# Two queue edits in a decoder layer: mixed rows split inside the output projection, operand differences started at the last scaling

## The chip, the cores and the metric

The kernel runs on one core of a Trainium2 chip. The metric is the device time of one execution in microseconds (us); lower is better. The core has five engines with a queue each, and each runs its queue in order: TensorE (PE in the profile) for matmuls, VectorE (DVE) and ScalarE (ACT) for elementwise work, GpSimd (POOL) for elementwise work in SBUF, and SyncE (SP), which here issues the DMAs.

## The reference

One layer of a hybrid decoder with D = 1024, run on 1024 prompt positions and 64 sampled ones (1088 rows together). Four retention heads and four mLSTM heads share one input projection; their gated outputs are concatenated, projected, normalised and added to the residual; a gated feed-forward part with a causal convolution of width 3 follows.

```python
proj = (rmsnorm(x, pre_mix_g) @ w_in).astype(f32)     # q, k, v, gates of both head groups
...
ret_y = head_groupnorm(ret_out, ret_g) * jax.nn.silu(g_r)
ml_y = head_groupnorm(ml_out, ml_g) * jax.nn.sigmoid(o_m)
mix = jnp.concatenate([ret_y, ml_y], axis=-1) @ w_out
x = x + rmsnorm(mix, post_mix_g)
h2 = rmsnorm(x, pre_ffn_g)
up = h2 @ w_up                                        # 2 * D_FF = 5632 columns
padded = jnp.concatenate([conv_buf, up], axis=1)
conv = sum(padded[:, j:j + L] * conv_w[j] for j in range(CONV_W)) + conv_b
gate, val = conv[..., :D_FF], conv[..., D_FF:]
ffn = (jax.nn.gelu(gate, approximate=True) * val) @ w_down
x = x + rmsnorm(ffn, post_ffn_g)
```

All inputs and outputs are float32. The states of both head groups and the convolution rows are outputs too.

## The kernel before

Rows are kept transposed: 128 features on the partitions, rows along the free axis. The 1088 rows are cut into four quarters of 272, numbered 0 to 3, and every matmul of the large projections has 128x128 weights and 272 columns. Each product is done in three matmuls: operand and weight are split into a high part (a copy rounded to a shorter float, on ACT) and a low part (the difference, on DVE), and high times high, low times high and high times low are summed in PSUM. `split_to` writes one ACT and one DVE instruction for that (profile lines L144 and L146), and leaves them in `last["split"]`.

The order of the instructions on each engine comes from a scheduler that places them by the order of the program and by when it thinks their operands are ready. `tc.issue_after(ins)` forces what is written inside it behind `ins` on that instruction's engine. Tiles with one tag share their space: a new one waits until every reader of the old one is done.

**From the mixer to the output projection.** The eight heads' results lie in `yT` (four tiles of two heads each, tags f0 to f3). The last four input projections make the late gates; `late_gate` multiplies a gate into `yT` (L497, the sigmoid L499, the product L500). With the last of them, `last_gate(b)` runs after each quarter b: it splits the finished rows of `yT` into the operand `mx` (`mix_split`, four ACT and four DVE instructions a quarter, tiles `mh` and `ml`), and at b = 1 and b = 3 it loads and splits the first two weight tiles of the output projection. Then the pools of the mixer are closed, and new tiles take their space.

`out_proj(b)` runs the output projection of one quarter: eight tiles of 128 features (`m` = 0 to 7), each with 24 matmuls (L165, tile `out`). `load_wo` loads and splits one weight tile ahead of each, with two more ahead of the first. The result is evacuated by ACT into `mo` (L861, which takes the tags f0 to f3 of `yT`), its square is summed into `oacc` (L863 on ACT, L865 on DVE). After each of the eight a step from a list is run: between the groups of one quarter the norm, the residual and the scaling of the quarter before are written (`post_mix`: `first`, two `residual`, `scale`). `rstd_block` is a norm: a matmul with ones over the partitions (L192, tiles `ssqb_po` and `ssqb_pf`), then L193 to L198 on DVE and ACT. `scale` multiplies eight tiles of a quarter by the norm (L899).

**The up-projection.** The first two column blocks (`PLAIN` = 2, j = 0 and 1) are done as plain products of the four quarters (`plain`, L1070 to L1072), in an order written by hand that is shown at the end of the code; the other 20 blocks use a Strassen form with seven products for eight (`product`, names A11, A12, S1 to S4, A22; L1026 to L1028). Its operands are the four parts of the scaled rows, B1 to B4 (by feature half and row half), and four combinations, T1 to T4. `first_half` and `second_half` split B1, B2 and B4, B3. `combine(i, eng)` writes the differences in place in `mo`, for one half of the columns each (L915 to L918): `combine(0, gpsimd)` has all four on POOL, `combine(1, vector)` has two on DVE and two on POOL. T2, T1, T3 and T4 are then split from `mo`. The result of block j goes into two tiles U (`Ug`, `Uv`), by L1011, L1000 and L1004 out of PSUM; `pair_out` runs the convolution over them (`conv`, L1034 to L1041, into tile `c`, which takes the space of the `mo` tile that T2 is split from), the gelu and the product. There are two sets of U tiles, so block j + 2 waits for the convolution of block j. Eight PSUM banks serve all products in turn.

Four products of the third block (A11 and A12, two column halves each) are run ahead and held in PSUM, until the U tiles of the first block are free. `weight_prep(j)` loads and splits the weights of block j; four pairs of weight tiles go round.

Of the kernel before, what the change touches and what calls it, by code (L numbers as in the profile page):

```python
# [10 lines left out]
F32 = mybir.dt.float32  # L11
# [3 lines left out]
ALU = mybir.AluOpType  # L15

P = 128
# [24 lines left out]
V_PREMIX, V_POSTMIX, V_PREFFN, V_POSTFFN, V_HEAD = 0, 8, 16, 24, 32  # L42
# [50 lines left out]
def hybrid_layer_kernel(ctx: ExitStack, tc: tile.TileContext, a: dict, o: dict):  # L93
    nc = tc.nc
# [8 lines left out]
    last = {}  # L103

    cp = pool("cp", bufs=1)
# [4 lines left out]
    def slot(i, name, dt=F32R):  # L110

        return (bigp if i < 8 else fp).tile([P, 4, 2 * Q], dt, tag=f"x{i}", bufs=1, name=name)

    def quadrants(name, th):

        return [tuple(slot(4 * th + 2 * kh + i, f"{name}{'hl'[i]}_{th}{kh}") for i in range(2)) for kh in range(2)]

    def qcols(b):
        return slice(Q * (b % 2), Q * (b % 2) + Q)
# [6 lines left out]
    def bank(p, cols, name, rows=P, dt=F32):  # L126
        t = p.tile([P, 512], dt, tag="bank", name=name)
        return t[:rows, :cols]
# [12 lines left out]
    def split_to(x, hi, lo, eng=nc.vector, after=None):  # L141
        act, dve = after or (None, None)
        with tc.issue_after(act.ins) if act else nullcontext():
            act = nc.scalar.activation(hi, x, AF.Copy)  # L144
        with tc.issue_after(dve.ins) if dve and eng is nc.vector else nullcontext():
            last["split"] = act, eng.tensor_tensor(lo, x, hi.bitcast(F32), ALU.subtract)  # L146
        return hi, lo

    def load_w(src, name, p=None, tag="w"):
        return split_w(stage_w(src, name), name, p, tag)  # L150
# [29 lines left out]
    vec = cp.tile([P, V_N], F32, name="vec")  # L180
# [36 lines left out]
    def xcols(b):  # L217
        o0, n = BLK[b]
        return a["x"][:, KT * o0:KT * (o0 + n)].rearrange("p (k n) -> p k n", k=KT)
# [560 lines left out]
    def mix_split(b, after=None):  # L780
        if b % 2 == 0:
            mx.append(quadrants("m", b // 2))
        o0, n = BLK[b]
        for k in range(0, KT, 2):
            hi, lo = (t[:, k % 4:k % 4 + 2, qcols(b)] for t in mx[b // 2][k // 4])
            x = yT[k // 2][:, :, o0:o0 + n]
            split_to(x, hi, lo, nc.vector, after)
# [6 lines left out]
    def last_gate(b):  # L794
        if b in (1, 3):
            wo.append(load_w(a["wo"][b // 2], f"out{b // 2}"))
            after = last["split"]
        for i in ((0,), (1,), (), (2, 3))[b]:
            mix_split(i, after if i > 1 else None)

    proj((31, late_gate(7)), done=last_gate)
    log_exp_tables(last["sigmoid"])
# [29 lines left out]
    def load_wo():  # L832

        m = len(wo)
        if m >= KT:
            return
        if m in (4, 6):
            wx.extend(slot(m + 4 + i, f"wo{'hl'[i]}{m}").rearrange("p k n -> p (k n)") for i in range(2))
        if m not in (4, 5):
            st = stage_w(a["wo"][m], f"out{m}")  # L840
        else:
            st = utile(f"st_out{m}", 0)[:, :D]
            nc.sync.dma_start(st, a["wo"][m])
        if m < 4:
            wo.append(split_w(st, f"out{m}", *wtile()))
        else:
            wo.append(split_to(st, *(t[:, m % 2 * D:(m % 2 + 1) * D] for t in wx[-2:])))
# [4 lines left out]
    def out_proj(b, steps=()):  # L852
        steps = list(steps)
        t = ttile(f"oacc{b}")
        acc, *sq = (t[:, i * Q:(i + 1) * Q] for i in range(3))
        for i in range(KT):
            m = (i + 4 * (b == 3)) % KT
            load_wo()
            ps = bank(psA, Q, f"out{m}_{b}")
            dense(ps, wo[m], mx, b)  # L860
            nc.scalar.activation(quarter(m // 4, b)[:, m % 4, :], ps, AF.Copy,  # L861
                                 scale=vec[:, V_POSTMIX + m:V_POSTMIX + m + 1])
            last["sq"] = nc.scalar.activation(sq[i % 2] if i else acc, ps, AF.Square)  # L863
            if i:
                last["acc"] = nc.vector.tensor_tensor(acc, acc, sq[i % 2], ALU.add)  # L865
            if steps:
                steps.pop(0)()
        for f in steps:
            f()
        return [acc, *sq]  # L870

    def post_mix(b, t):

        xr, st = [], {}

        def first():
            for kh in range(2):
                x = slot(6 + kh, f"xr{kh}_{b}", F32).rearrange("p k n -> p (k n)") if b == 3 else utile(f"xr{kh}_{b}", 1)
                x = x[:, :4 * Q].rearrange("p (k n) -> p k n", k=4)
                nc.sync.dma_start(x, xcols(b)[:, 4 * kh:4 * kh + 4, :])  # L880
                xr.append(x)
            st["r"] = t[1]
            rstd_block(t[0], t[1], t[2], t[0], f"po{b}", last.get("fill"))

        def residual(kh):
            m = quarter(kh, b)
            nc.vector.tensor_tensor(m, m, st["r"].unsqueeze(1).broadcast_to([P, 4, Q]), ALU.mult)
            (nc.gpsimd if kh and b == 3 else nc.vector).tensor_tensor(m, m, xr[kh], ALU.add)
            nc.scalar.activation(xr[kh], m, AF.Square)
            nc.sync.dma_start(x1cols(b)[:, 4 * kh:4 * kh + 4, :], m)  # L890
            nc.vector.tensor_tensor(xr[kh][:, :2], xr[kh][:, :2], xr[kh][:, 2:], ALU.add)

        def scale():
            nc.vector.tensor_tensor(xr[0][:, :2], xr[0][:, :2], xr[1][:, :2], ALU.add)
            nc.vector.tensor_tensor(xr[0][:, 0], xr[0][:, 0], xr[0][:, 1], ALU.add)
            rstd_block(xr[0][:, 0], t[1], t[2], t[0], f"pf{b}", last.get("fill"))
            for k in range(KT):
                m = quarter(k // 4, b)[:, k % 4, :]
                nc.vector.scalar_tensor_tensor(m, m, vec[:, V_PREFFN + k:V_PREFFN + k + 1], st["r"],  # L899
                                               ALU.mult, ALU.mult)  # L900

        return [first, lambda: residual(0), lambda: residual(1), scale]

# [8 lines left out]

    def combine(i, eng):
        q = {(kh, th): mo[kh][th][:, :, qcols(i)] for kh in range(2) for th in range(2)}
        eng.tensor_tensor(q[0, 0], q[0, 1], q[0, 0], ALU.subtract)  # L915
        nc.gpsimd.tensor_tensor(q[0, 1], q[1, 1], q[0, 1], ALU.subtract)
        eng.tensor_tensor(q[1, 1], q[1, 1], q[0, 0], ALU.subtract)
        nc.gpsimd.tensor_tensor(q[1, 0], q[1, 0], q[1, 1], ALU.subtract)  # L918
# [12 lines left out]

    skip = lambda: None
    spaced = lambda f: [f[0], skip, f[1], f[2], skip, f[3]]
    acc = out_proj(0)
    acc = out_proj(1, spaced(post_mix(0, acc)))
    acc = out_proj(2, spaced(post_mix(1, acc)) + [lambda: first_half(0)])
    acc = out_proj(3, spaced(post_mix(2, acc)) + [lambda: first_half(1)])


    cache = fp.tile([P, 2 * JT, 9, 2], F32, bufs=1, name="cache")  # L940
    nc.sync.dma_start(cache, a["cache"].rearrange("p (j s t) -> p j s t", j=2 * JT, s=9))
    seq = lambda v: v.rearrange("p (s t) -> p s t", s=NB)

    def weight_prep(j):

        plain = j < PLAIN
        ws = {}

        def parts(i, x, *names):
            p, tag = wtile()  # L950
            n = len(names) * D // 2
            hi = p.tile([P, D], F32R, tag=tag + "hi", name=f"wh_up{j}_{i}")[:, :n]
            lo = p.tile([P, D], F32R, tag=tag + "lo", name=f"wl_up{j}_{i}")[:, :n]
            split_to(x, hi, lo, nc.vector, (last["sq"], last["acc"]) if i in (1, 2) else None)
            for c, name in enumerate(names):
                cols = slice(c * D // 2, (c + 1) * D // 2)
                ws[name] = hi[:, cols], lo[:, cols]

        parts(0, stage_w(a["wu"][j, 0], f"up{j}_0"), "A11", "A12")
        if plain:  # L960
            parts(3, stage_w(a["wu"][j, 1], f"up{j}_1"), "A22", "A21")
            yield ws
            return
        yield ws
        sums = sd[j].rearrange("p b n -> p (b n)")
        for i, names in ((1, ("S1", "S2")), (2, ("S4", "S3"))):
            parts(i, stage_w(sums[:, (i - 1) * D:i * D], f"up{j}_{i}"), *names)
            yield
        st = fp.tile([P, D // 2], F32, tag="s1", bufs=1, name=f"st_up{j}_3")
        nc.sync.dma_start(st, a["wu"][j, 1][:, :D // 2])  # L970
        parts(3, st, "A22")
        yield
# [255 lines left out]
    acc = [t_acc[b // 2][:, b % 2 * Q:(b % 2 + 1) * Q] for b in range(4)]  # L1228
# [171 lines left out]
```

## Time and profile before

| what | value |
|---|---|
| median of three runs | 1375.17 us (1373.82 to 1376.09) |
| the profiled execution | 1375.41 us, of it 1373.6 us from the first to the last instruction |
| PE busy | 1348.8 us, 98% of the span |
| DVE, ACT, POOL busy | 1009.7, 596.3, 440.8 us (74%, 43%, 32%) |
| mean granted TensorE clock | 0.993 |
| last input projection ends, output projection starts | 541.05 and 541.67 us |
| output projection ends, first plain product starts | 646.56 us |
| first held product of the third block | 700.58 us |

Busy time of PE counts pipelined matmuls from start to end, so that it can be near 100% while matmuls start at different rates; the granted clock tells slow ones from fast ones. In the rows of instructions, the first number is the start in us after the first instruction, the second the time from the start of the first to the end of the last of the group, `xN` their number, and a bracket tells how long the engine was idle before and what released it. In the rows of waits stand the waiting engine and line, what it waited for, and total us, times and the longest.

### The profile page before, as it was taken

How to read it: one execution, taken by the hardware profiler on the slowest of the kernel's cores; microseconds unless marked ns; L12 is line 12 of the kernel's file. 1: busy time of each engine (PE TensorE's matmuls, PEld its weight loads, DVE VectorE, ACT ScalarE, POOL GpSimd, SP SyncE). 2: the span in 40 equal slices, each digit the busy share in tenths (PEclk: the TensorE clock that was granted, in tenths of full speed). 3: DMA queues.
4: the chain of work that ended last, by engine and by line, in shares of the span. 5: the costliest groups of instructions: out<-in, count | busy, mean ns of one | idle time of the engine just before them, and what ended most of it. 6: DMA issues, size and time to landing. Idle time of an engine off the chain costs nothing.

```text
span 1373.6 us, 26916 instructions
## 1 busy us (share of the span) xinstructions
PE 1348.8 (98%) x10583; PEld 1323.9 (96%) x10583; DVE 1009.7 (74%) x2013; ACT 596.3 (43%) x1107; POOL 440.8 (32%) x567
## 2 busy tenths in 40 slices
PE   9999999999999999999999999999999999999995
PEld 8999999999999999999899999999999999999995
DVE  6778775556465366568899978778778789995677
ACT  8444433212222235446364434434344455453652
POOL 0344440577775000000353322221222205872000
PEclk9999999999999999999999999999999999999998
DMA  6433442478784211432123444443444359533363
GB/s 242 134 113 123 159 156 64 157 212 192 227 186 156 64 34 48 158 116 97 64 93 135 163 143 136 135 132 116 142 150 141 135 158 334 175 95 95 92 212 130
DMA packets 93166, 192.80 MB, mean 140 GB/s; under 512 B 16240, under 2 KB 41456, under 8 KB 92528
## 3 DMA queue, kind: packets, MB, share of 16 engines
q1 hardware_dynamic: 80736, 149.03, 33.2%
q0 software_dynamic: 12160, 41.95, 10.7%
q8 instruction: 83, 1.36, 0.4%
q14 instruction: 43, 0.35, 0.1%
q10 hardware_dynamic: 144, 0.11, 0.0%
HBM read 134.58 MB, written 56.47 MB: 139 GB/s over the span
## 4 chain that ended last, share of the span: by engine, by line
PE 90%; DVE 4%; ACT 3%; DMA 1%; issue 1%; SPq 0%; DVEq 0%; ACTq 0%
PE in L165 27%; PE up_S L1028 6%; PE out L165 6%; PE up_S L1027 6%; PE up_S L1026 6%; PE dn L1223 5%; PE dn L1225 5%; PE dn L1224 4%; PE up_A L1027 4%; PE up_A L1026 4%; PE up_A L1028 4%; ACT hh L205 1%; PE up_A L1071 1%; PE up_A L1072 1%; PE up_A L1070 1%
## 5 line engine op out<-in xcount | busy, mean ns | idle before, releaser
L165 PE MATMUL in<-hh,wh_in 128*128 128x272 f32 x1024 | 299.7, 294 | 1.7 <-ACT v_r L453 1.5
L165 PE MATMUL in<-hh,wl_in 128*128 128x272 f32 x1024 | 295.9, 291 | 0.0
L165 PE MATMUL in<-hl,wh_in 128*128 128x272 f32 x1024 | 295.2, 291 | 0.0
L165 PEld LDWEIGHTS in<-hh,wh_in 128*128 128x128 f32 x1024 | 192.3, 188 | 5.8 <-issue 2.0
L165 PEld LDWEIGHTS in<-hh,wl_in 128*128 128x128 f32 x1024 | 192.2, 189 | 3.8 <-issue 3.5
L165 PEld LDWEIGHTS in<-hl,wh_in 128*128 128x128 f32 x1024 | 191.7, 188 | 1.6 <-issue 1.5
L144 ACT ACTIVATE wh_up<-st_up 128x1024 fp32r<-128x1024 f32 x84 | 80.6, 960 | 160.6 <-PE up_S L1027 98.3
L146 DVE TENSOR_TENSOR wl_up<-st_up,wh_up 128x1024 fp32r<-128x1024 f32 x84 | 95.8, 1141 | 8.9 <-ACT wh_up L144 8.9
L1000 DVE TENSOR_TENSOR Uv<-Uv,up_S 128x272 f32<-128x272 f32 (+1 forms) x200 | 66.4, 374 | 46.1 <-PE up_S L1028 46.1
L1152 DVE TENSOR_TENSOR rb<-rb 128x544 fp32r<-128x544 f32 x78 | 74.3, 957 | 34.2 <-ACT rb L1151 33.7
L736 POOL TENSOR_TENSOR tab<-tab 128x256 f32<-128x256 f32 x104 | 84.1, 819 | 9.3 <-DMA tab<-in_wu 4.7
L1172 POOL TENSOR_TENSOR wd<-wd 128x512 f32<-128x512 f32 x44 | 72.3, 1669 | 34.6 <-DMA wd<-in_wd 20.8
L1151 ACT ACTIVATE rb<-rb 128x544 fp32r<-128x544 f32 x78 | 50.5, 650 | 74.3 <-DMA rb<-bd 70.2
L1056 POOL TENSOR_TENSOR act<-act 128x544 f32<-128x544 f32 x40 | 63.1, 1577 | 61.0 <-DMA bd<-act 33.1
L991 POOL MEMSET Ug<- 128x2 f32 x22 | 2.2, 100 | 234.4 <-DMA xr<-in_x 121.8
L1041 DVE SCALAR_TENSOR_TENSOR c<-Uv,vec,c 128x1024 f32<-128x1024 f32 (+1 forms) x88 | 70.0, 798 | 9.1 <-ACT c L1039 9.1
L1041 DVE SCALAR_TENSOR_TENSOR c<-Ug,vec,c 128x1024 f32<-128x1024 f32 x88 | 67.5, 805 | 1.2 <-ACT c L1039 1.2
L736 POOL TENSOR_TENSOR wq<-wq 128x256 f32<-128x256 f32 x56 | 50.3, 908 | 48.3 <-DMA wq<-in_wu 46.1
L1039 ACT ACTIVATE c<-Ug,vec 128x1024 f32<-128x1024 f32 (+1 forms) x44 | 34.6, 834 | 53.6 <-DVE Ug L1004 47.4
L736 POOL DMA_DIRECT2D tab<-in_wu x52 | 36.8, 714 | 61.7 <-DVE k_r L468 44.0
L146 DVE TENSOR_TENSOR wl_in<-st_in,wh_in 128x1024 fp32r<-128x1024 f32 (+2 forms) x33 | 40.5, 1226 | 13.5 <-ACT wh_in L144 13.4
L1028 PE MATMUL up_S<-T1h,wl_up 128*128 128x272 f32 x160 | 46.4, 290 | 0.0
(548 smaller groups left out, 4668.0 us busy)
## 6 DMA issues: line engine op xcount, KB each, us to landing
rb<-bd SPq DMA_DIRECT2D x76, 272.0 KB, 2.9
st_up<-sd SPq DMA_DIRECT2D x40, 512.0 KB, 4.0
bd<-act SPq DMA_DIRECT2D x33, 544.0 KB, 3.9
st_in<-in_wi SPq DMA_DIRECT2D x31, 512.0 KB, 3.8
tab<-in_wu POOLq DMA_DIRECT2D x52, 256.0 KB, 4.6
sd<-tab POOLq DMA_DIRECT2D x26, 512.0 KB, 3.5
st_up<-in_wu SPq DMA_DIRECT2D x24, 512.0 KB, 3.3
wd<-in_wd SPq DMA_DIRECT2D x44, 256.0 KB, 4.8
```

The lines of the kernel that those rows point to most:

```text
L144: act = nc.scalar.activation(hi, x, AF.Copy)
L146: last["split"] = act, eng.tensor_tensor(lo, x, hi.bitcast(F32), ALU.subtract)
L165: nc.tensor.matmul(ps, u[:, ws], v, start=k == i == 0, stop=k == KT - 1 and i == 2)
L736: last["sums"] = f(*args)
L1026: nc.tensor.matmul(ps, wh[:, c], xh[:, k, n], start=k == 0, stop=False)
L1027: nc.tensor.matmul(ps, wh[:, c], xl[:, k, n], start=False, stop=False)
L1028: nc.tensor.matmul(ps, wl[:, c], xh[:, k, n], start=False, stop=k == 3)
L1041: nc.vector.scalar_tensor_tensor(c, u(i), cw(i), c, ALU.mult, ALU.add)
L1152: nc.vector.tensor_tensor(lo, x, hi.bitcast(F32), ALU.subtract)
L1172: nc.gpsimd.tensor_tensor(quad(p, out), quad(p, x), quad(p, y), op)
L1223: nc.tensor.matmul(t, wh[:, ms], ah, start=k == 0, stop=False)
L1225: last["dn"] = nc.tensor.matmul(t, wl[:, ms], ah, start=False, stop=k == KH - 1)
```

## The change

The splits of the mixed rows of quarters 2 and 3 are taken out of `last_gate`. They become steps of `out_proj(0)`: quarter 2 after its first group of 24 matmuls, by when five weight tiles of the output projection have been written in the program, and behind the last of their splits on ACT and DVE; quarter 3 after its third group, with no order forced. `last_gate` keeps the splits of quarters 0 and 1 and the loads of two weight tiles.

`scale` of the last quarter now leaves its last scaling in `last["acc"]`, and is followed by one instruction on POOL, over one column of a tile `hold`, that reads the last scaled rows (`last["gate"]`). The first difference of `combine(0)` is ordered behind that instruction on POOL, the first of `combine(1)` behind the last scaling on DVE; the splits that were ordered behind `last["acc"]` and are written later (B4 and B3 of the second column half, T1 to T4, and weights of the third and later blocks) now stand behind the last scaling too, instead of the last sum of `out_proj(3)`.

The weight splits of block j = 1 are ordered behind the last square of `out_proj(3)` on ACT and its last sum on DVE.

No matmul, DMA or split is added or taken away; one small POOL instruction is added.

```diff
     def last_gate(b):
         if b in (1, 3):
             wo.append(load_w(a["wo"][b // 2], f"out{b // 2}"))
-            after = last["split"]
-        for i in ((0,), (1,), (), (2, 3))[b]:
-            mix_split(i, after if i > 1 else None)
+        if b < 2:
+            mix_split(b)
...
             for k in range(KT):
                 m = quarter(k // 4, b)[:, k % 4, :]
-                nc.vector.scalar_tensor_tensor(m, m, vec[:, V_PREFFN + k:V_PREFFN + k + 1], st["r"],
-                                               ALU.mult, ALU.mult)
+                d = nc.vector.scalar_tensor_tensor(m, m, vec[:, V_PREFFN + k:V_PREFFN + k + 1], st["r"],
+                                                   ALU.mult, ALU.mult)
+            if b == 3:
+                last["acc"] = d
+                last["gate"] = nc.gpsimd.tensor_tensor(hold, m[:, :1], m[:, 1:2], ALU.subtract)
...
     def combine(i, eng):
         q = {(kh, th): mo[kh][th][:, :, qcols(i)] for kh in range(2) for th in range(2)}
-        eng.tensor_tensor(q[0, 0], q[0, 1], q[0, 0], ALU.subtract)
+        with tc.issue_after(last["gate" if eng is nc.gpsimd else "acc"].ins):
+            eng.tensor_tensor(q[0, 0], q[0, 1], q[0, 0], ALU.subtract)
...
-    acc = out_proj(0)
+    acc = out_proj(0, [lambda: mix_split(2, last["split"]), skip, lambda: mix_split(3)])
...
+    hold = cp.tile([P, 1], F32, name="hold")
...
-            split_to(x, hi, lo, nc.vector, (last["sq"], last["acc"]) if i in (1, 2) else None)
+            split_to(x, hi, lo, nc.vector, (last["sq"], last["acc"]) if i in (1, 2) or j == 1 else None)
```

The hand-written order behind which the differences stand:

```python
for j in range(PLAIN):
    begin_plain(j)
plain(*firsts[0], 0)
norm()
second_half(0)
plain(*firsts[0], 1)
add0()
add1()
plain(*firsts[0], 2)
plain(*firsts[1], 0)
scale()
second_half(1)
plain(*firsts[1], 1)
plain(*firsts[1], 2)
for f in firsts:
    plain(*f, 3)
...
held = [product(name, i) for name in ("A11", "A12") for i in range(2)]
for i, e in ((0, nc.gpsimd), (1, nc.vector)):
    combine(i, e)
```

## The prediction

> **What bounds the kernel now.** I read the page first (busy shares, the chain), then who PE waited for, then the stretches round the two places of the edit, then the instructions of DVE, ACT and POOL there.
>
> ```profile
> span 1373.6 us, 26916 instructions
> PE 1348.8 (98%) x10583; PEld 1323.9 (96%) x10583; DVE 1009.7 (74%) x2013; ACT 596.3 (43%) x1107; POOL 440.8 (32%) x567
> PE 90%; DVE 4%; ACT 3%; DMA 1%; issue 1%; SPq 0%; DVEq 0%; ACTq 0%
> ```
>
> PE is the bound, and the chain of waits runs over it. So a change elsewhere can only give back what PE loses near it: its waits, and the slow matmuls behind them. PE's waits between 500 and 720 us, and stretches (columns: length, then busy us and count of PE, PEld, DVE, ACT, POOL, granted clock, DMA share, GB/s):
>
> ```profile
> PE out L165 <- ACT wh_out L144: 2.6, 2, 2.1
> PE ssqb_po L192 <- DVE oacc L865: 2.3, 2, 1.8
> PE ssqb_pf L192 <- DVE xr L895: 1.1, 1, 1.1
> ...
> 541.60:573.75 32.15, 29.46 (x216) 28.91 (x216) 0.95 0.47 171
> ...
> 652.70:662.65 9.95, 8.15 (x51) 7.87 (x51) 6.71 (x8) 2.04 (x5) 5.61 (x2) 0.83 0.33 107
> 674.80:682.50 7.70, 6.64 (x51) 6.47 (x51) 6.00 (x12) 3.76 (x7) 0.00 (x0) 1.00 0.01 3
> 700.00:745.00 45.00, 45.00 (x361) 45.00 (x361) 44.90 (x70) 26.96 (x37) 18.18 (x29) 1.00 0.42 144
> 880.00:960.00 80.00, 80.00 (x640) 80.00 (x640) 63.25 (x117) 34.15 (x44) 18.13 (x39) 1.00 0.41 133
> ```
>
> Undisturbed, PE starts a matmul every 80.00/640 = 0.125 us. The 216 of the first stretch need 27.0 us and took 32.1: 5.1 us lost, 2.6 of it waiting and 2.5 in slow matmuls (mean clock 0.95). The second holds one group of 48 and the two of a norm: 50 × 0.125 = 6.25 against 9.95, so 3.7 lost, 1.8 waiting and 1.9 at clock 0.83. The third loses 7.70 − 6.25 = 1.45. These three, 10.2 us, are all that the edit can win.
>
> **First part: splits of the later quarters' mixed rows moved into the output projection.** ACT and DVE now stand so (start, length):
>
> ```profile
> 541.67 0.36 PE L165 MATMUL out<-mh,wh_out 128*128 128x272 f32 x1 [0.62 <-DVE z L497]
> 542.05 3.93 ACT L144 ACTIVATE mh<-yT 128x544 fp32r<-128x544 f32 x7
> 548.93 1.99 ACT L144 ACTIVATE wh_out<-st_out 128x1024 fp32r<-128x1024 f32 x2
> 543.32 4.53 DVE L146 TENSOR_TENSOR ml<-yT,mh 128x544 fp32r<-128x544 f32 x7
> 547.77 0.43 DVE L500 TENSOR_TENSOR yT<-yT,z 128x272 f32<-128x272 f32 x1
> 543.43 0.33 SPq L132 DMA_DIRECT2D st_out<-in_wo  x1
> 548.34 0.80 SPq L843 DMA_DIRECT2D st_out<-in_wo  x2
> 552.11 1.06 ACT L144 ACTIVATE woh<-st_out 128x1024 fp32r<-128x1024 f32 x1 [0.61 <-DMA st_out<-in_wo]
> ```
>
> The third and fourth weight tile (wh_out at 548.93) are behind seven splits on ACT, and the last gate product L500, after which the space of the next stage is free, is behind seven on DVE. Take them away and L500 runs 4.4 us earlier, near 543.4; the third weight's high half then ends at about 545.0 (1.06 each), and PE wants it at 541.67 + 48 × 0.125 = 547.7. The fourth has its load issued at 543.43 as before; the loads of the fifth and sixth leave at 543.9 instead of 548.34, land 3.8 later (548.34 to 552.11) and are wanted from 553.7 on. SP issues the same DMAs, those behind the two (rows of x, the cache, more weights) earlier too; they meet the fourth weight's load, which is ahead in the same queue. So both waits go: **−5.1**. The eight splits themselves (3.93/7 = 0.56 on ACT, 4.53/7 = 0.65 on DVE, each) land under 216 matmuls, where DVE has room. What is late next is the first evacuation into the mo tiles, which take the space of the mixed rows and so wait for these splits, until about 556; PE has eight PSUM banks and asks for the first again only at 541.67 + 192 × 0.125 = 565.7. Ends for this part: −5.1 and, if another weight half is late by a split pair, −2.6.
>
> **Second part: POOL's differences held back, weight splits of j = 1 behind the last sum.**
>
> ```profile
> 644.93 5.68 DVE L899 SCALAR_TENSOR_TENSOR mo<-mo,vec,oacc 128x272 f32<-128x272 f32 x8
> 646.74 2.73 POOL L915 TENSOR_TENSOR mo<-mo,mo 128x1088 f32<-128x1088 f32 x1 [5.71 <-DVE mo L899]
> 652.93 1.21 DVE L146 TENSOR_TENSOR wl_up<-st_up,wh_up 128x1024 fp32r<-128x1024 f32 x1
> 654.07 0.43 DVE L865 TENSOR_TENSOR oacc<-oacc 128x272 f32<-128x272 f32 x1
> 656.97 3.46 POOL L916 TENSOR_TENSOR mo<-mo,mo 128x1088 f32<-128x1088 f32 x1 [7.49 <-DVE B4l L146]
> 660.51 2.54 POOL L917 TENSOR_TENSOR mo<-mo,mo 128x1088 f32<-128x1088 f32 x1
> 661.62 1.72 DVE L197 SCALAR_TENSOR_TENSOR oacc<-oacc 128x272 f32<-128x272 f32 x1 [3.24 <-ACT oacc L196]
> 663.38 2.66 DVE L198 SCALAR_TENSOR_TENSOR oacc<-oacc 128x272 f32<-128x272 f32 x1
> 675.98 0.70 PE L192 MATMUL ssqb_pf<-xr,ones 128*128 128x272 f32 x2 [1.06 <-DVE xr L895]
> 679.64 0.44 DVE L198 SCALAR_TENSOR_TENSOR oacc<-oacc 128x272 f32<-128x272 f32 x1
> 680.12 3.39 DVE L899 SCALAR_TENSOR_TENSOR mo<-mo,vec,oacc 128x272 f32<-128x272 f32 x8
> ```
>
> The sum L865 that PE waits for stands behind eight scalings that took 5.68 instead of the 3.39 of the second row of the same kind, because POOL's L915 ran among them, and behind one weight split (1.21). Both go: L865 ends near 654.5 − 2.3 − 1.2 = 651.0, PE wants it at 652.6. The chain behind it loses POOL's L917 and L918 (L197 1.72 and L198 2.66, where the next norm's L198 has 0.44) and a split of T2 between; it ends some 3 us before its norm is reached. Both waits and the slow matmuls go: −3.7 − 1.45 = **−5.15**. The held-back weight splits are wanted only behind three groups of 48, 18 us later, and cost nothing while that cover lasts. The new gate instruction is one element a lane.
>
> The price is behind the last scaling:
>
> ```profile
> 686.05 3.46 POOL L916 TENSOR_TENSOR mo<-mo,mo 128x1088 f32<-128x1088 f32 x1 [13.87 <-DVE B4l L146]
> 689.54 1.29 DVE L917 TENSOR_TENSOR mo<-mo,mo 128x1088 f32<-128x1088 f32 x1 [2.43 <-POOL mo L916]
> 690.75 1.28 DVE L146 TENSOR_TENSOR T3l<-mo,T3h 128x1088 fp32r<-128x1088 f32 x1
> 692.02 3.58 DVE L146 TENSOR_TENSOR T2l<-mo,T2h 128x1088 fp32r<-128x1088 f32 x1
> 690.92 3.54 POOL L918 TENSOR_TENSOR mo<-mo,mo 128x1088 f32<-128x1088 f32 x1 [1.41 <-DVE mo L917]
> 696.00 1.57 ACT L1039 ACTIVATE c<-Ug,vec 128x1024 f32<-128x1024 f32 x2 [2.58 <-POOL cache L1034]
> 706.12 0.28 DVE L1041 SCALAR_TENSOR_TENSOR c<-Uv,vec,c 128x64 f32<-128x64 f32 x1
> 707.28 0.69 ACT L1011 ACTIVATE Uv<-up_A 128x272 f32<-128x272 f32 x2
> 688.55 0.41 PE L1070 MATMUL up_A<-B4h,wh_up 128*128 128x272 f32 x2
> 741.46 0.83 DVE L1004 TENSOR_TENSOR Ug<-Uv,up_S 128x272 f32<-128x272 f32 x3
> ```
>
> From the end of the scaling (683.5) DVE works 22.9 us to the end of the first convolution (706.4). The convolution writes into the space of the tile that T2 is split from, so it starts when T2's split is done (695.6, ACT at 696.0). Only then are the U tiles free, ACT evacuates the first held product (707.3 to 707.6), and PE has a bank for S4, due 192 matmuls after 688.55, at 712.55: 5.0 us to spare. Now the scaling ends at about 677.9 (ssqb_pf at 671.2, 3.3 of norm without T3's split between, 3.39), and S4 is due at 712.55 − 5.15 = 707.4. But POOL's four operations of the first half (2.5 each) and two splits (T2, T3, 1.28 each) are added to DVE's crowded stretch, and DVE and POOL exclude each other: T2l took 3.58 instead of 1.28 beside L918, L198 2.66 instead of 0.44. Where they stood, the four cost DVE 2.3 (scalings) + 1.3 (L197) + 2.2 (L198) + 0 (L916 at 657, while DVE waited 3.24 for ACT) = 5.8; all four in full are 10.2. I take 10.1, since after 700 DVE is busy 44.90 of 45 us and has no gap for them; both ends stay in the range. The held product's evacuation: 677.9 + 22.9 + 10.1 + 2.6 + 0.9 = 714.4, PE's stop 714.4 − 707.4 = **+7.0**, in one piece or in several (the weights of the held products, T2 and T1 are on the way). A stop costs slow matmuls too: 1.9 as at 652.70, **+1.8 to 1.9**. At the low price of 5.8 the stop is 2.7.
>
> [...]
>
> **The sum:** −5.1 − 5.15 + 7.0 + 1.85 = −1.4 us. The profiled execution took 1375.41 (span 1373.6 and 1.8 around it), 0.24 above the median of 1375.17: 1374.0 in its terms, **1373.8** as a median. 0.2% (2.75 us) is about what a measurement here can tell from no change: that is within it.
>
> **The rivals.**
> - Faster: POOL's four fit where DVE waits anyway, as the L916 at 657 did. For it: DVE waited 2.43 for POOL at 687, and the queues are ordered anew. Against it: DVE has no pause after 690. Price 5.8: −10.25 + 2.7 + 1.9 = −5.6, **1369.6**; without a slow clock 1367.7.
> - Slower: DVE stays the bound and PE stops several times, each time with slow matmuls: first for the weights of the held products (their split queued behind L917, which waits for POOL's fifth operation), then at S4, then later, because DVE cannot recover: the evacuation at 741.46 ends 741.9 and its bank is due two groups of 14 products and two products (30 × 12 × 0.125 = 45.0) behind the held ones' start at 688.55 + 96 × 0.125 = 700.55, at 745.55, so spare time falls from 5.0 to 3.7, 1.3 more. Price: 7.0 + 1.3 + 3 × 1.9 = 14.0, so +3.7, **1378.9**. It decides from stops of 13 us on. For it: three needs come due within 12 us. Against it: slow matmuls give DVE time to catch up.
> - The first part does not do what it says: a weight tile still late by its load. Then −2.6 instead of −5.1: 1376.3. Against it: a load lands 3.8 us after its issue, and each has over 1 us to spare. It is counted half with no change, half with slower.
>
> **How the numbers follow.** Forecast 0.36 (1371 to 1377 by itself), faster rival 0.38 with its milder forms, slower 0.18, the undone first part 0.08. Faster by over 0.2%: 0.38; within: 0.40; slower: 0.22. The range reaches from the faster rival without slow clock to a little beyond the slower one, 1367.7 to 1380.0; outside lie one in ten at each end at most. The forecast is the likeliest single size; faster is nearly as likely.
>
> **What would show it.** The first part is right if PE no longer waits for wh_out at 550 and the stretch from the first out product over 216 matmuls is about 27 us at clock 1.00; wrong if that wait stands. The second is right if both ssqb waits are gone and the eight scalings at 645 take 3.4. The price is right if POOL's L915 to L918 stand behind the last scaling, T2l and T3l take over 3 us there, and PE waits some 7 us in all between 690 and 720 with a clock below 1; if PE shows no such wait, the faster rival is true and the time is near 1367. What would make it wrong at the root: DVE splits reordered so that the first convolution is not behind POOL's chain.

## Result and the profile after

| | before | changed |
|---|---|---|
| median of 11 runs each, us | 1375.38 | 1378.69 |
| lowest to highest, us | 1373.61 to 1378.98 | 1377.34 to 1381.01 |
| span of the profiled execution, us | 1373.6 | 1376.0 |

The ratio of changed to before is 1.0024, 95% interval 1.0015 to 1.0032: 3.3 us slower (the two profiled executions lie 2.4 apart). The forecast was 1373.8, 1.4 faster; the time lies in the range (1367.7 to 1380.0), but the sign was wrong.

The page of the changed kernel, span and busy shares:

```profile
span 1376.0 us, 26902 instructions
...
PE 1348.7 (98%) x10583; PEld 1324.4 (96%) x10583; DVE 1010.7 (73%) x2013; ACT 595.6 (43%) x1107; POOL 442.3 (32%) x568
```

The work is the same as before, PE's included; what differs is when it is done. Who PE waited for (us in total, times, longest). Line numbers behind the edit have moved by up to four: the sum that was L865 is L864, the scaling L899 is L898, the evacuation L1011 is L1015, the differences L915 to L918 are L918 to L921.

```profile
PE up_S L1030 <- ACT Uv L1015: 5.1, 1, 5.1
PE up_A L1032 <- DVE wl_up L146: 2.5, 1, 2.5
...
PE out L165 <- DVE z L497: 1.0, 1, 1.0
...
PE ssqb_po L192 <- DVE oacc L864: 0.5, 1, 0.5
```

The two waits for wh_out are gone, and so are the long wait for the sum and the one for the next norm. In their place stand two that before did not have: for a weight's low half (wl_up), ahead of the held products, and for an evacuation on ACT (L1015), ahead of S4. The stretches that answer to those of before, and those behind the new waits (columns as in the prediction):

```profile
541.50:568.75 27.25, 27.18 (x216) 27.21 (x217) 16.29 (x23) 17.19 (x31) 0.67 (x4) 1.00 0.56 202
647.60:653.95 6.35, 6.35 (x52) 6.27 (x50) 4.38 (x6) 2.03 (x5) 0.00 (x0) 1.00 0.54 168
666.12:672.45 6.33, 6.33 (x51) 6.25 (x50) 4.10 (x10) 3.14 (x6) 0.00 (x0) 1.00 0.00 0
690.55:700.00 9.45, 6.92 (x43) 6.71 (x42) 7.90 (x5) 3.54 (x6) 9.45 (x7) 0.82 0.33 111
...
712.25:720.00 7.75, 7.71 (x39) 7.71 (x40) 7.75 (x10) 3.31 (x5) 4.38 (x2) 0.60 0.54 171
720.00:745.00 25.00, 25.00 (x202) 25.00 (x201) 24.34 (x46) 10.91 (x13) 8.21 (x17) 1.00 0.41 142
```

The first three run at full clock and without a wait: 216 matmuls in 27.25 us where 32.15 stood, and the two stretches round the norms 6.35 and 6.33 where 9.95 and 7.70 stood. The fourth and fifth are the price: in the 7.75 us behind S4's start PE, never idle, started 39 matmuls where 62 fit, at a granted clock of 0.60. From 720 on the pitch is 0.125 us again.

PE's first matmul of each stretch gives the balance. I use lengths, since the start of the first one, ahead of the edit, lies anywhere from 541.3 to 544.1 in the profiled executions of all kernels here.

| from … to | before | changed | difference | forecast |
|---|---|---|---|---|
| first out product (541.67; 541.57) to first plain product (646.56; 641.55) | 104.89 | 99.98 | −4.91 | −5.1 |
| to the first held product (700.58; 690.70) | 54.02 | 49.15 | −4.87 | −5.15 |
| to the T2 product of the next block (727.6; 730.17) | 27.0 | 39.5 | +12.45 | +8.85 |
| sum | | | +2.7 | −1.4 |

The rest of the span adds nothing. So the whole question lies in the third row: 7.59 of the 12.45 are the two waits (2.52 and 5.07), the other 4.86 slow matmuls. What ran there in the changed kernel, DVE, POOL, ACT, SP and PE, from the timeline:

```profile
669.68 3.39 DVE L898 SCALAR_TENSOR_TENSOR mo<-mo,vec,oacc 128x272 f32<-128x272 f32 x8
...
681.75 3.63 DVE L920 TENSOR_TENSOR mo<-mo,mo 128x1088 f32<-128x1088 f32 x1 [5.08 <-POOL mo L919]
686.56 3.58 DVE L146 TENSOR_TENSOR T2l<-mo,T2h 128x1088 fp32r<-128x1088 f32 x1
690.06 3.51 DVE L146 TENSOR_TENSOR wl_up<-st_up,wh_up 128x1024 fp32r<-128x1024 f32 x1
...
698.67 2.10 DVE L146 TENSOR_TENSOR wl_up<-st_up,wh_up 128x1024 fp32r<-128x1024 f32 x1 [1.55 <-ACT wh_up L144]
...
711.47 0.27 DVE L1045 SCALAR_TENSOR_TENSOR c<-Uv,vec,c 128x64 f32<-128x64 f32 x1
...
673.21 3.51 POOL L902 TENSOR_TENSOR hold<-mo 128x1 f32<-128x1 f32 x1 [13.14 <-DVE mo L898]
676.69 2.54 POOL L918 TENSOR_TENSOR mo<-mo,mo 128x1088 f32<-128x1088 f32 x1
679.19 5.04 POOL L919 TENSOR_TENSOR mo<-mo,mo 128x1088 f32<-128x1088 f32 x2
685.46 3.54 POOL L921 TENSOR_TENSOR mo<-mo,mo 128x1088 f32<-128x1088 f32 x1 [1.23 <-DVE mo L920]
688.93 3.56 POOL L920 TENSOR_TENSOR mo<-mo,mo 128x1088 f32<-128x1088 f32 x1
...
697.57 1.06 ACT L144 ACTIVATE wh_up<-st_up 128x1024 fp32r<-128x1024 f32 x1 [3.94 <-DMA st_up<-sd]
711.84 0.69 ACT L1015 ACTIVATE Uv<-up_A 128x272 f32<-128x272 f32 x2 [0.76 <-DVE c L1045]
...
693.60 0.33 SPq L132 DMA_DIRECT2D st_up<-sd  x1
...
693.63 0.39 PE L1032 MATMUL up_A<-B1h,wl_up 128*128 128x272 f32 x1 [2.52 <-DVE wl_up L146]
712.29 0.59 PE L1030 MATMUL up_S<-B3h,wh_up 128*128 128x272 f32 x1 [5.07 <-ACT Uv L1015]
```

Read down, this is the chain. The last scaling ends at 673.07. DVE makes one difference and two splits, then finds its next difference (L920) behind POOL's L919 and idles 5.08; before it idled 2.43 there. POOL comes to that L919 late: the gate instruction took 3.51 and L918 2.54 ahead of it. Three DVE operations take 3.5 to 3.6 instead of 1.2 to 1.3, each beside a POOL difference: L920, T2l, and wl_up beside the L920 at 688.93. That wl_up is what PE stands for at 691.1. The load of S2's and S1's weights, which needs a staging buffer of that kind, leaves at 693.60, right behind its end at 693.57, and ACT waits 3.94 for it with T1's split and the convolution queued behind; DVE in turn idles 1.55 for ACT's half of that weight split. The last piece of the convolution ends at 711.74, ACT evacuates, and S4 starts at 712.29.

### The profile page after: what moved, and what is told of

The parts are those of the page before. It is cut to its first block, busy times and chain, and to the rows that moved or that the text cites. A ratio compares the mean times of both kernels' runs of the same rounds, so it can differ in the third digit from the quotient of the medians.

```text
span 1376.0 us, 26902 instructions
## 1 busy us (share of the span) xinstructions
PE 1348.7 (98%) x10583; PEld 1324.4 (96%) x10583; DVE 1010.7 (73%) x2013; ACT 595.6 (43%) x1107; POOL 442.3 (32%) x568
## 4 chain that ended last, share of the span: by engine, by line
PE 88%; DVE 5%; DMA 2%; ACT 2%; issue 2%; POOL 0%; SPq 0%; DVEq 0%; ACTq 0%; POOLq 0%
PE in L165 27%; PE out L165 6%; PE up_S L1030 5%; PE up_S L1032 5%; PE up_S L1031 5%; PE dn L1227 5%; PE dn L1229 5%; PE dn L1228 5%; PE up_A L1031 4%; PE up_A L1030 4%; PE up_A L1032 4%; DMA wd<-in_wd 1%; ACT hh L205 1%; PE s_m L600 1%; PE us_m L664 1%
## 5 line engine op out<-in xcount | busy, mean ns | idle before, releaser
L146 DVE TENSOR_TENSOR wl_up<-st_up,wh_up 128x1024 fp32r<-128x1024 f32 x84 | 99.2, 1182 | 10.6 <-ACT wh_up L144 10.6
L1030 PE MATMUL up_S<-B3h,wh_up 128*128 128x272 f32 x160 | 47.4, 296 | 5.1 <-ACT Uv L1015 5.1
```

The costliest lines, as they stand in the source:

```text
L1030: nc.tensor.matmul(ps, wh[:, c], xh[:, k, n], start=k == 0, stop=False)
```

## Experiments

Each was timed beside the kernel before. In place means from the first out product to the first plain one, and from there to the first T4 product of the third block, both in the profiled execution: 104.89 and 72.07 before, 99.98 and 79.60 changed.

| kernel | median, us | before beside it | ratio, 95% interval | in place, us |
|---|---|---|---|---|
| e1_part1 | 1371.04 | 1374.91 | 0.9969 [0.9956, 0.9981] | 100.04, 71.70 |
| e2_part2 | 1382.84 | 1374.91 | 1.0061 [1.0048, 1.0074] | 105.83, 79.48 |
| e3_nogate | 1372.17 | 1374.91 | 0.9983 [0.9972, 0.9993] | 101.01, 71.20 |
| e4_drop | 1367.87 | 1374.91 | 0.9952 [0.9938, 0.9966] | 101.56, 67.18 |
| e5_dve | 1370.08 | 1375.69 | 0.9958 [0.9944, 0.9971] | 100.12, 69.86 |
| e6_dve_early | 1367.78 | 1375.69 | 0.9943 [0.9931, 0.9956] | 100.45, 67.47 |
| e7_busy | 1381.20 | 1374.67 | 1.0052 [1.0036, 1.0068] | 99.98, 83.2 |
| e8_alldve | 1367.03 | 1374.67 | 0.9944 [0.9930, 0.9958] | 100.05, 67.46 |
| e9_zeros | 1376.37 | 1375.11 | 1.0009 [1.0000, 1.0018] | 100.81, 76.81 |

### Each part alone: e1_part1 and e2_part2

e1 is the kernel before with the first part only:

```diff
-        for i in ((0,), (1,), (), (2, 3))[b]:
-            mix_split(i, after if i > 1 else None)
+        if b < 2:
+            mix_split(b)
...
-    acc = out_proj(0)
+    acc = out_proj(0, [lambda: mix_split(2, last["split"]), skip, lambda: mix_split(3)])
```

> Only the first part is done: the mixed rows of quarters 2 and 3 are split inside the output projection, all else as before. If the two parts act each for itself, the two waits for weight tiles near 550 us and the slow matmuls behind them go, and nothing is paid for it: 4.9 us less than before, about 1370.5. If the gain of the first part only moves PE ahead of work that then holds it (POOL and DVE behind the output projection), part of it comes back as a wait later: 1372 to 1375.

e2 is the kernel before with everything else of the change (the gate and its instruction, the differences behind it, `or j == 1`).

> Only the second part is done: the differences held back behind the last scaling, the weight splits of j = 1 behind the last sum; the mixed rows as before. If the parts act each for itself: both norm waits gone (4.9 us less), two stops behind the last scaling with their slow matmuls (12.4 us more), so 7.5 us more than before, about 1383. If the stops come from both parts together, because the first brings PE there earlier than weights and loads allow: about as before, 1374 to 1377.

Alone, the first part gives 3.9 us and the second costs 7.9. Their sum, +4.0, is near the +3.3 of both: within the intervals the parts add up. PE's waits in e2 between 500 and 760 us show the same two stops as the changed kernel, so they belong to the second part:

```profile
PE up_S L1031 <- ACT Uv L1016: 5.1, 1, 5.1
PE up_A L1033 <- DVE wl_up L146: 2.5, 1, 2.5
PE out L165 <- ACT wh_out L144: 2.4, 2, 2.1
```

In e1 out to plain is 4.85 shorter, as in the changed kernel. The wait for the next norm rose from 1.06 to 2.26, while the 1.80 us for the sum was this time not followed by slow matmuls; the last section returns to that.

### The gate taken away: e3_nogate

```diff
-                last["gate"] = nc.gpsimd.tensor_tensor(hold, m[:, :1], m[:, 1:2], ALU.subtract)
...
-        with tc.issue_after(last["gate" if eng is nc.gpsimd else "acc"].ins):
-            eng.tensor_tensor(q[0, 0], q[0, 1], q[0, 0], ALU.subtract)
+        eng.tensor_tensor(q[0, 0], q[0, 1], q[0, 0], ALU.subtract)
```

> The changed kernel without the order on the first difference of each combination: POOL may start its four operations of the first half as early as before; the small POOL instruction is gone; the splits stay behind the last scaling. If the price is that of POOL's four operations in the crowded stretch: both stops there go (12.4 us), some of the norm waits return (1 to 4), so about 1368 to 1370. If the price is that of the splits that now stand behind the last scaling (T2, T3): the stops stay for the most part, 1374 or more.

The stops between 690 and 715 go, and the waits at the norms come back. PE's waits at the norms and DVE in the timeline of e3:

```profile
PE ssqb_pf L192 <- DVE xr L894: 2.9, 1, 2.9
PE ssqb_po L192 <- DVE oacc L864: 1.1, 2, 0.7
...
642.20 5.68 DVE L898 SCALAR_TENSOR_TENSOR mo<-mo,vec,oacc 128x272 f32<-128x272 f32 x8
...
658.06 2.66 DVE L198 SCALAR_TENSOR_TENSOR oacc<-oacc 128x272 f32<-128x272 f32 x1
660.75 4.72 DVE L886 TENSOR_TENSOR mo<-mo,oacc 128x1088 f32<-128x1088 f32 x2
```

The scalings take 5.68 again, L198 2.66, and the two residual products 4.72 where e6 below, without POOL there, has 2.50. PE waits 2.87 for the next norm and 0.67 for the sum. So what else the second part does (e3 has it, e1 does not: above all the weight splits behind the last sum) shortens the one wait by 1.1 and lengthens the other by 0.6. The gate and the order behind it cost 8.4 from plain to T4 (79.60 against 71.20), with what they save at the norms already counted; the ratios differ by 5.6 us, in part because out to plain is 1.0 longer in e3. The median of 1372.17 lies between the two ranges expected: the stops went, as in the first, but the two norm waits remained.

### The four differences left out, and given to DVE: e4_drop, e5_dve, e6_dve_early, e8_alldve

```diff
e4:
-    for i, e in ((0, nc.gpsimd), (1, nc.vector)):
+    for i, e in ((1, nc.vector),):
e5 (in combine, then at its calls):
-        nc.gpsimd.tensor_tensor(q[0, 1], q[1, 1], q[0, 1], ALU.subtract)
+        rest = nc.gpsimd if i else eng
+        rest.tensor_tensor(q[0, 1], q[1, 1], q[0, 1], ALU.subtract)
...
-    for i, e in ((0, nc.gpsimd), (1, nc.vector)):
+    for i, e in ((0, nc.vector), (1, nc.vector)):
e6 (as e5, but called in scale(), ahead of the last norm's own DVE work):
+            if b == 3:
+                last["acc"] = s
+                combine(0, nc.vector)
...
-    for i, e in ((0, nc.gpsimd), (1, nc.vector)):
+    for i, e in ((1, nc.vector),):
e8 (as e6, the second half too):
-        rest = nc.gpsimd if i else eng
+        rest = eng
```

> The changed kernel without the differences of the first column half (four POOL operations left out, so T1 to T4 of that half are split from rows that were not subtracted); order, splits and matmuls as in the changed kernel. If POOL's holding DVE up in the crowded stretch is the price: no stop, no slow clock there, both gains kept, about 1366. If the price lies in the splits, in the late load of a weight tile or in the new order: PE still waits 5 us or more between 690 and 715, 1371 to 1376.

> The changed kernel with the four first-half differences wholly on VectorE, in place behind the last scaling; the second half's two and two as before. Theory (the loss comes from VectorE being held out by GpSimd's operations, 5.1 us idle and 3.5 us for a two-tensor operation alone beside another): four operations of about 2.35 us (half of 4.72, the price of two beside GpSimd; alone somewhat less) replace four GpSimd ones that cost VectorE more than that, the weights of S2 and S1 come in time, the stops are smaller or gone: 1368 to 1373. Rival (VectorE has too much work there, whoever holds the differences): four operations add 8 to 9 us to VectorE's queue ahead of S4, the stops stay or grow: 1377 or more.

> The changed kernel with the four first-half differences wholly on VectorE, issued while the last quarter's norm is on its way (behind the last sum of squares, ahead of the norm's own VectorE work), where VectorE waits for the column sums. Theory (place on VectorE's queue decides): two to three of the four fit into the idle time of the norm, no GpSimd lock at the start of the splits, no stop in 690 to 715: 1367 to 1371. Rival (the norm's chain is put back by the operations that do not fit, 5 us or more, and PE's products of the last quarter wait): 1374 or more, with a new wait ahead of the products of the last quarter.

> The kernel of e6_dve_early with the second half's four differences on VectorE as well, so that GpSimd makes none. In e6 PE no longer waits between 560 and 760, but VectorE still idles 2.57 us for a GpSimd difference and one two-tensor operation takes 3.58 us beside another. Theory (only waits of PE count, and none is left there): same time as e6, 1367 to 1368.5, though VectorE's queue gets 2 to 3 us ahead. Rival (some of what is left over PE's pitch hangs on VectorE's lead in this stretch): 1 us or more below e6, under 1366.8. Second rival (two more operations of 1.29 us on VectorE bring a stop back): 1369.5 or more.

Without the four, plain to T4 is 67.18, 12.4 less than in the changed kernel, as much as it loses there by the third row of the balance: all of that hangs on them. But they need not cost that. e5, with the same work at the same place on DVE, loses 2.7 of 12.4, and e6, with the work earlier on DVE, 0.3: it costs no more than leaving the work out. DVE in the timelines of e5 and then of e6:

```profile
675.34 2.49 DVE L918 TENSOR_TENSOR mo<-mo,mo 128x1088 f32<-128x1088 f32 x2
...
680.15 1.29 DVE L920 TENSOR_TENSOR mo<-mo,mo 128x1088 f32<-128x1088 f32 x1
681.47 4.87 DVE L921 TENSOR_TENSOR mo<-mo,mo 128x1088 f32<-128x1088 f32 x2
```

```profile
656.91 2.50 DVE L886 TENSOR_TENSOR mo<-mo,oacc 128x1088 f32<-128x1088 f32 x2
...
666.56 1.28 DVE L921 TENSOR_TENSOR mo<-mo,mo 128x1088 f32<-128x1088 f32 x1
667.88 1.29 DVE L923 TENSOR_TENSOR mo<-mo,mo 128x1088 f32<-128x1088 f32 x1
669.75 0.44 DVE L193 TENSOR_SCALAR oacc<-ssqb_pf 128x272 f32<-128x272 f32 x1 [0.58 <-PE ssqb_pf L192]
670.11 1.28 DVE L924 TENSOR_TENSOR mo<-mo,mo 128x1088 f32<-128x1088 f32 x1
671.42 1.29 DVE L925 TENSOR_TENSOR mo<-mo,mo 128x1088 f32<-128x1088 f32 x1
673.05 0.44 DVE L197 SCALAR_TENSOR_TENSOR oacc<-oacc 128x272 f32<-128x272 f32 x1 [0.34 <-ACT oacc L196]
673.53 0.44 DVE L198 SCALAR_TENSOR_TENSOR oacc<-oacc 128x272 f32<-128x272 f32 x1
```

A difference takes DVE 1.29 us when POOL is quiet, and POOL 2.52 to 2.54. Beside one on POOL a DVE operation of 1.28 took 3.58 (T2l in the changed kernel): held up by 2.30, nearly twice the time in which DVE would do the difference itself. In e6 two of the four run while DVE waits for PE's column sums and two while it waits for ACT. My expectation of e5 put the four at 2.35 each, from two that had POOL beside them; the quiet ones took 1.29, but two of e5's DVE differences still stood beside one of POOL's and took over 3.6 (one is in the 4.87 above). e8 shows that once PE has no wait left, DVE's remaining 2.57 us idle (e6, for POOL's L923) is worth nothing that can be told: 0.9944 against 0.9943. e6 and e8 beat both kernels, by 7.9 and 7.6 us of the kernel before, and no wait over 1 us is left to PE from 500 to 760.

### Slow matmuls, with PE kept busy: e7_busy and e9_zeros

```diff
e7, behind S1's second group:
+        for f in range(38):
+            nc.tensor.matmul(ps, ws["S1"][1][:, :P], X["T1"][0][:, 0, qcols(1)], start=f == 0, stop=f == 37)
e9, at the end of S1's second group, in its own accumulation:
+    FILL = 38
...
+                more = FILL if (j, name, i) == (PLAIN, "S1", 1) else 0
...
+            for f in range(more):
+                nc.tensor.matmul(ps, wl[:, :P], zeros, start=False, stop=f == more - 1)
```

> The changed kernel with 38 more matmuls, behind S1's second group of the held block, into a bank of their own that nothing reads: 4.75 us at the pitch of 0.125, which keep PE busy during most of its 5.07 us wait for Uv ahead of S4, and which nothing but S4's matmuls stands behind. Theory (the slow matmuls behind the wait, 24 of S4 in 5.60 us instead of 3.0, come from PE having been idle): S4 starts when it did, at full clock; about 2.6 us less than the changed kernel, 1376, and the granted clock in the 7.75 us behind S4's start goes from 0.60 to nearly 1. Rival (the slow matmuls have another cause, for instance the rate of VectorE or the transfers): no gain, 1378.7, and the clock there stays near 0.6.

> What e7_busy was meant to do, without a bank of its own: 38 matmuls of a weight tile with a tile of zeros (written by GpSimd long before) end the accumulation of S1's second group of the held block, 4.75 us at the pitch of 0.125. They add zeros, need no free bank, and keep PE busy during most of the 5.07 us that S4 waits for its bank, whose last reader is ScalarE's eviction at 711.84. Theory (S4's slow matmuls, 24 in 5.60 us instead of 3.0, come from PE having been idle): S4 starts when it did, at full clock: 2.6 us less than the changed kernel, 1376, the granted clock behind S4's start near 1 instead of 0.60. Rival (another cause): 1378.7 and 0.60. Second rival (S1's result, out 4.75 us later, puts S4's evictions back): 1380 or more. What the first stop of 2.5 us costs in slow matmuls (1.8 us in the changed kernel, nothing in e7_busy) can differ from run to run and can move any of these by up to 1.8.

e7 missed its aim. PE's waits in it between 500 and 760 us:

```profile
PE fill L1124 <- ACT Uv L1015: 6.0, 1, 6.0
PE up_A L1032 <- DVE wl_up L146: 2.5, 1, 2.5
```

The filling matmuls themselves waited for ACT's evacuation: all eight banks were in use, the new one was the one that S4 would have had, and that is the bank of the first held product. The 38 matmuls came on top of the wait instead of into it, +3.9 us against the changed kernel by the two ratios. What it shows is that S4's stop is a bank that is not given back.

e9 needs no bank, and its S4 starts after a wait of 0.51. That wait, and the stretch behind that start, as long as the one in the changed kernel:

```profile
PE up_S L1033 <- ACT Uv L1018: 0.5, 1, 0.5
...
714.50:722.25 7.75, 7.73 (x61) 7.73 (x62) 7.75 (x13) 4.37 (x6) 3.89 (x2) 1.00 0.37 113
```

61 matmuls at clock 1.00 instead of 39 at 0.60, with DVE as busy (7.75) as there. Plain to T4 is 2.8 shorter than in the changed kernel, the time 1376.4, as expected; the two ratios lie 2.1 us apart, and their intervals just touch. The stop at the held products was followed by slow matmuls in both (17 and 18 starts, last section), so it does not make the difference. The DMAs moved less here (113 GB/s against 171), but 202 stood beside full clock in the first stretch of the changed kernel. So here it was the idle time of PE (5.07 us against 0.51) that made the matmuls behind it slow, not the traffic beside them, and the stop of 5.07 us cost some 8.0 (5.07 + 23 × 0.125).

## Why the prediction was wrong

- **First part, −5.1.** Right: −4.91 in place. Both waits for wh_out went, the 216 matmuls took 27.2 us at clock 1.00, and no later weight tile was late in this trace. In e3, e4 and e9, which have this part too, PE waited 0.6 to 1.0 near 560 for the low half of a weight tile (wol), and out to plain took 0.8 to 1.6 more. The rival in which this part is undone is out; e1 shows it by itself.
- **Second part's gain, −5.15.** Right: −4.87. The scalings take 3.39, and the waits at both norms are gone.
- **S4's stop, +7.0.** Nearly right in size, 7.59, but in two pieces. The two errors in it cancel: from the last scaling's end to S4's start the sum had 714.4 − 677.9 = 36.5, the trace has 712.29 − 673.07 = 39.2; yet S4 came due 4.6 us later than reckoned, because PE had been stopped and slowed at the held products first. That the size is near is luck. The 2.7 extra are not in the two terms that I added (10.1 and 2.6). Two things came in that the sum put at nothing: the gate instruction, which took 3.51 on POOL ahead of the differences (DVE idled 5.08 behind them where it had idled 2.43), and the load behind the blocked weight split (ACT waited 3.94 for it, DVE 1.55 for ACT). I had named that split in the slower rival, but not that its buffer holds up the next load. Of the two splits that were to take over 3 us, T2l did and T3l did not (1.28); L920 and wl_up did.
- **Slow matmuls, +1.85. This is the step that failed.** I wrote "in one piece or several" and then charged one piece, at the price seen behind a wait of 1.80. Measured: 4.86. Behind the second stop 39 of 62 matmuls started in 7.75 us, 23 × 0.125 = 2.9 lost; that leaves about 2.0, nearly all at the first (the stretch from the first held product to the first T2 product grew from 6.01 to 10.34, 1.8 more than the wait of 2.52). The 3.0 between 4.86 and 1.85 make most of the 4.1 between +2.7 and −1.4; the waits' 0.6 and the two gains' 0.5 make the rest. The nearest row to a long stop stood in the prediction, in the first stretch, whose waits of 2.07 and 0.55 cost 2.5 us of slow matmuls: I took the smaller of two shown prices for the larger stop.
- **The rivals.** The slower one had the mechanism (stops at the weights of the held products, then at S4, each with slow matmuls) and 1378.9, against 1378.69 measured; its third, later stop did not come, and its waits were smaller. It had a chance of 0.18. Its condition, stops of 13 us on, was just missed at 12.45, and gains 0.5 below mine made that up. That the median came so near to its figure is partly luck: the profiled executions give +2.7 in place where it said +3.7. The faster one failed as the argument against it said: DVE has no pause for POOL's four. It came true with the work on DVE (e5, e6), which I had not thought of, although the trace showed a difference on DVE at 1.29 beside POOL's 2.54.

That PE's two stops stem from POOL's four operations is shown by e3, e4 and e5. How much of the 2.7 is the gate's and how much the late load's is read from the timeline and was not tried alone; e4, e5 and e6 keep the gate, so it makes no such stops without the four.

## What to carry to other kernels

Where two engines shut each other out, price an operation by what the other engine loses, not by the time it takes: moving a 2.5 us operation from the slow engine to the crowded one cost it less here (1.29) than being held out by it (2.30). And count a slow clock for each stop of PE that you forecast, not once for all of them, since the stop of 5.07 us cost nearly 8 here.

## What the runs showed of the hardware

**A wait of about 2 us is followed by slow matmuls in some traces and not in others.** Matmul starts and the granted clock in the 3.5 us behind each wait of PE between 1.8 and 2.9 us from 600 to 760 us (28 fit; 26 where the two longer matmuls of a norm are among them, as at 1.80, 2.26 and 2.87):

| kernel, end of the wait | wait, us | starts | clock |
|---|---|---|---|
| before, 654.55 | 1.80 | 14 | 0.53 |
| e1_part1, 651.03 | 1.80 | 26 | 1.00 |
| e1_part1, 672.10 | 2.26 | 26 | 1.00 |
| changed, 693.63 | 2.52 | 18 | 0.63 |
| e2_part2, 699.21 | 2.53 | 17 | 0.59 |
| e9_zeros, 695.86 | 2.53 | 17 | 0.57 |
| e7_busy, 694.56 | 2.53 | 27 | 1.00 |
| e3_nogate, 672.38 | 2.87 | 26 | 1.00 |

The same instruction after the same 2.53 us ran at half rate for some 3 us in e9 and at full rate in e7. At the last norm of the kernel (ssqb_fin, near 1350) ten of the traces have another wait of 2.02 to 2.39: seven were followed by 14 to 19 starts, three (e2, e6, e7) by 26 at clock 1.00. None of the 24 waits between 0.9 and 1.6 us in the eleven traces (past the first 15 us) was followed by a clock below 1.00. The 5.07 us of the changed kernel and of e2 were both followed by 6 us at 4 to 5 starts per us, the 6.02 of e7 by 15 starts in 3.5 us and the full rate after that. So the 1.9 that the prediction took for a short stop is the price in the bad case, not the mean. What decides between the two is not shown by these runs.

**The smallest POOL operation took 3.5 and 5.9 us beside DVE's.** The gate instruction reads two columns and writes one. It took 3.51 us in the changed kernel (quoted above), and in e4, where DVE's operations stood closer:

```profile
677.13 5.92 POOL L902 TENSOR_TENSOR hold<-mo 128x1 f32<-128x1 f32 x1 [13.69 <-DVE mo L898]
```

It ended only when DVE paused, behind five operations in a row; in the changed kernel it ended behind the difference and the two splits that DVE made first (672.99 to 676.67). I had called it one element a lane and given it no price.
